# A decoder trunk in one kernel: a depthwise convolution split between TensorE and VectorE, a swish without GpSimd, and modulation work moved to an earlier stage

## The chip, the cores and the metric

The kernel runs on one core of one Trainium2 chip. The metric is the device time of one launch in microseconds (us), here the median of the runs of one kernel. TensorE (PE in the rows, its weight loads PEld) multiplies, VectorE (DVE), ScalarE (ACT) and GpSimd (POOL) do the elementwise work, and SyncE (SP) issues nearly all DMA transfers.

## The reference

The sequence has 256 tokens of 2048 channels. Layer 0 mixes tokens with a state-space mixer (S5), layer 1 with a Conformer convolution; a SwiGLU network of width 5632 follows each. Every sub-layer gets its shift, scale and gate from a projection of one conditioning vector `c` (the modulation).

```python
for i in range(DEPTH):                                   # 2 layers
    mod = c_act @ ada_w[i] + ada_b[i]                    # 2048 x 12288: six vectors of 2048
    h = x * (1.0 + sc_m) + sh_m
    y = s5_mixer(h, ...) if i % 2 == 0 else conv_mixer(h, ...)
    x = layer_norm(ALPHA * x + (1.0 + gt_m) * y, ...)
    h = x * (1.0 + sc_f) + sh_f
    y = swiglu_ffn(h, ffn_w_gu[i], ffn_w_down[i])
    x = layer_norm(ALPHA * x + (1.0 + gt_f) * y, ...)

def conv_mixer(u, w_pw1, w_dw, b_dw, g_norm, b_norm, w_pw2):
    ab = u @ w_pw1
    v = ab[..., :d] * jax.nn.sigmoid(ab[..., d:])
    v = depthwise causal convolution of v, 31 taps per channel, + b_dw
    v = layer_norm(v, g_norm, b_norm)                    # over the channels
    return jax.nn.silu(v) @ w_pw2
```

## The kernel before

**Units.** Every weight matrix goes through the same path (class `Unit`, `gemm`). A unit is 1 MB of weights, 4 blocks of 128 rows by 512 columns, loaded by SyncE into one of four `raw` buffers. ScalarE casts it to `whi` (L830) and VectorE subtracts to get the remainder `wlo` (L831); both have two buffers. TensorE then runs 24 products of 512 columns (L884) or 48 of 256 columns (L888), those with `whi` first and those with `wlo` last. A unit's casts can start when the unit two places earlier has been multiplied.

**Modulation.** `AdaQueue` works through the 2048 x 12288 matrices beside the units: at each unit `ada.rate` is added to a credit, and at 1.0 one step is taken: a load of 1 MB into another `raw` buffer (L684) and a multiply-add of 128 x 2048 on VectorE (L699). `ada.hold` stops it. There are 128 such steps in all.

**The convolution stage** multiplies by `cv_w_pw1` in eight groups of four units; group i gives channel chunks 2i and 2i+1 (128 channels each). Group 0 is done by `entry.panel`, groups 1 to 7 by `gemm`. When a group is ready, `conv_in` writes it zero-padded to `pad`, sends it to a scratch in DRAM (L1542) and reads it back four times shifted (`vs`, L1557); GpSimd makes the tap matrices `lw` (L1547). `conv_out` (L1574) computes a chunk with 32 products of 256 columns; fp32 products have two instructions each in the trace, so 64 rows a chunk. VectorE takes the result from PSUM to `V`, with the bias added and a shift subtracted (L1583). The last group has no time for DRAM: `conv_spread` (L1564) copies and shifts it with TensorE, into PSUM banks that ScalarE (L1566) and VectorE (L1568) empty in turn. Spreads and convolutions share three banks (tag `aux`). What is to run some units later is put into a list (`later.put(n, ...)`, n units ahead).

**Normalisation and swish.** `Stats` sums `V` and its squares (`lnsq`) over the chunks on VectorE (L773, L775), and `finish` sums over the partitions on TensorE (`lnsum`). Then `Feed` runs beside the first product with `cv_w_pw2` (q = 0, four units, L888): for each pair of chunks `swish` normalises on VectorE (L818, L819), takes the sigmoid and the affine on ScalarE (L1611, L945), multiplies on GpSimd (L1613), rounds to the high part on VectorE (L908) and takes the low part on GpSimd (L909). TensorE waits for these parts pair by pair.

The instructions of each engine are put in a fixed order when the program is built, and each engine works through its own in that order.

Of the kernel before, what the change touches and what calls it, by code (L numbers as in the profile page):

```python
# [26 lines left out]
CONV_G = 8  # L27
WIDTH = 31
# [477 lines left out]
def kernel(  # L506
# [231 lines left out]
    class Stats:  # L738
# [22 lines left out]
        def add(self, i, z):  # L761

            sq = self.sp.tile([P, 2, SEQ], F32, tag="lnsq", name="lnsq", bufs=2)
            act = nc.scalar.activation(out=sq, in_=z, func=AF.Square)
# [7 lines left out]
            a, b = self.first if i == 1 else (s[:, 0], s[:, 1])  # L772
            dve = nc.vector.tensor_tensor(out=s[:, 0], in0=a, in1=z, op=ADD)  # L773
            if i < 7:
                nc.vector.tensor_tensor(out=s[:, 1], in0=b, in1=sq, op=ADD)  # L775
            else:
                self.tail = sq
                self.marks = [dve, act]

        def finish(self, fill=None):  # L780
# [4 lines left out]
            sp, s, sq = self.sp, self.s, self.tail  # L785
# [5 lines left out]
            for k in range(2):  # L791
                for q in range(4):
                    t = slice(64 * q, 64 * q + 64)
                    mm = nc.tensor.matmul(b[32 * q:32 * q + 32, 64:P], ones[:, 0:32], sq[:, k, t], start=False, stop=k == 1)
# [567 lines left out]
    const2 = wp = ln_col = wtap = fold32 = row_of = None  # L1362

# [71 lines left out]
    def load_vectors():  # L1435
# [18 lines left out]
        later.put(4, lambda: turn_vectors(ab, ln, rt))  # L1454

# [20 lines left out]
    with mctx:  # L1476
# [39 lines left out]
        ada.rate, ada.behind = 0.71, True  # L1516
# [11 lines left out]
        for p in pad:  # L1528
            nc.vector.memset(p[:, :, :WIDTH - 1], 0.0)
            nc.vector.memset(p[:, :, LP - 1:], 0.0)  # L1530
        dramp = cvctx.enter_context(tc.tile_pool(name="dram", bufs=1, space=bass.MemoryType.DRAM))
        scr = [dramp.tile([P, 2, LP], F32, name=f"scr{i}") for i in range(7)]
        cstats = Stats("cln", sp)
        ada.rate = 0.6

        def conv_in(i, t):
            p = pad[i % 2]
            for k in range(2):
                nc.scalar.copy(out=p[:, k, WIDTH - 1:LP - 1].rearrange("p (c t) -> p t c", t=2), in_=t[:, k].rearrange("p (t c) -> p t c", t=2))
            vs = cp.tile([P, 2, 4, LS], F32, tag="vs", name="vs", bufs=2)  # L1540
            if i < 7:
                later.put(3, lambda: nc.sync.dma_start(scr[i], p))  # L1542
                later.put(4, lambda: conv_copies(scr[i], vs))
            for k in range(2):
                ch = 2 * i + k
# [23 lines left out]

        def conv_out(ch, vs, lw):  # L1570
            acc = aux("conv")[:, :SEQ]
            for g in range(CONV_G):
                for q in range(4):
                    nc.tensor.matmul(  # L1574
                        acc[32 * q:32 * q + 32, :], lw[:, q, g, :], vs[:, q, 4 * g:4 * g + SEQ], start=g == 0, stop=g == CONV_G - 1)
# [9 lines left out]
            if ch % 2 == 1:  # L1585
                cstats.add(ch // 2, V[:, ch - 1:ch + 1])
# [6 lines left out]
        def swish(i, r):  # L1593
            s2 = slice(2 * i, 2 * i + 2)
            if i == 0:
                h = sp.tile([P, 2, SEQ], F32, tag="hf", name="hf", bufs=2)
                for ch in range(2):
# [6 lines left out]
                    nc.gpsimd.tensor_tensor(out=hl[:, ch], in0=h[:, ch], in1=hh[:, ch].bitcast(F32), op=SUB)  # L1604
# [8 lines left out]
            nc.gpsimd.tensor_tensor(out=h, in0=h, in1=V[:, s2], op=MUL)  # L1613
# [64 lines left out]
```

## Time and profile before

| | before |
|---|---|
| median of 3 runs | 2331.22 us (2330.57 to 2331.48) |
| the profiled execution | 2333.25 us, of it a span of 2331.5 us |
| TensorE busy | 2258.8 us, 97% |
| VectorE busy | 1637.7 us, 70% |
| ScalarE, GpSimd busy | 1009.7 us and 234.6 us |
| convolution stage, groups 1 to 7 | about 1215 to 1417 us of the span |
| its last convolutions, sums | about 1417 to 1442 us |
| swish beside the first product with `cv_w_pw2` | about 1447 to 1487 us |
| first feed-forward network | about 420 to 1170 us |

All stretches below are microseconds from the start of the span. A row of the timeline has its start, its time (of a row with a count, from the first start to the last end), the engine, line, operation, what is written and read, and in brackets the idle time just before and what ended it. Instructions on VectorE and ScalarE overlap a little: three equal ones in a row take less than three times one.

### The profile page before, as it was taken

The numbers are of one execution on the slowest core, as the hardware profiler recorded it, in microseconds if no ns is written. First come the engines' busy times: TensorE is split into PE (matmuls) and PEld (weight loads), VectorE is DVE, ScalarE is ACT, GpSimd is POOL, SyncE is SP. The second block draws the span as 40 slices with busy tenths as digits, with TensorE's granted clock in tenths as the row PEclk, the third lists the DMA queues.
The fourth block names the chain that finished last, engine by engine and source line by source line (L and its number), as shares of the span: only waits on it lengthen the run. The fifth ranks groups of instructions, "written<-read, shape, count | busy, mean of one in ns | idle before, by whom it ended". The sixth has DMA issues, their size and how long they took to land.

```text
span 2331.5 us, 34014 instructions
## 1 busy us (share of the span) xinstructions
PE 2258.8 (97%) x13905; PEld 1818.0 (78%) x13905; DVE 1637.7 (70%) x1754; ACT 1009.7 (43%) x1242; POOL 234.6 (10%) x307
## 2 busy tenths in 40 slices
PE   7888999999999999999999998999999999999998
PEld 4545777888888888888887776797888888888888
DVE  8899888877776777777884656788755444455564
ACT  4665334644333333434463322556433433334343
POOL 5662000200000000000030111302000000000000
PEclk8999999999999999999999999999999999999999
DMA  9888898489888888988748886765865555555552
GB/s 334 300 295 294 293 334 293 163 307 320 298 320 295 311 314 305 323 294 304 271 145 243 260 244 213 264 218 182 279 225 181 194 185 193 186 181 190 188 164 90
DMA packets 382307, 582.36 MB, mean 250 GB/s; under 512 B 13603, under 2 KB 279123, under 8 KB 367683
## 3 DMA queue, kind: packets, MB, share of 16 engines
q1 hardware_dynamic: 381718, 579.73, 73.6%
q8 instruction: 109, 1.79, 0.3%
q0 software_dynamic: 192, 0.37, 0.1%
q14 instruction: 48, 0.39, 0.0%
q10 hardware_dynamic: 240, 0.08, 0.0%
HBM read 575.97 MB, written 4.15 MB: 249 GB/s over the span
## 4 chain that ended last, share of the span: by engine, by line
PE 76%; DVE 9%; issue 5%; DMA 4%; ACT 3%; POOL 2%; SPq 1%; DVEq 0%; POOLq 0%; ACTq 0%
PE acc L884 66%; PE acc L888 3%; PE conv L1574 2%; DVE wlo L831 2%; PE turned L900 2%; DMA raw<-in_s_w_glu_dram 1%; DVE pin L462 1%; ACT whi L830 1%; POOL h L982 1%; PE y L499 1%; DVE adaacc L699 1%; DMA raw<-in_cv_w_pw_dram 1%; DMA vs<-scr 1%; DVE x L450 1%; DVE pin L450 1%
## 5 line engine op out<-in xcount | busy, mean ns | idle before, releaser
L831 DVE TENSOR_TENSOR wlo<-raw,whi 128x2048 fp32r<-128x2048 f32 x344 | 797.7, 2319 | 510.1 <-ACT whi L830 510.0
L830 ACT CAST whi<-raw 128x2048 fp32r<-128x2048 f32 x344 | 654.8, 1904 | 806.2 <-PE acc L884 533.4
L884 PE MATMUL acc<-whi,h 128*128 128x512 f32 x3648 | 901.1, 396 | 15.7 <-ACT whi L830 15.3
L884 PEld LDWEIGHTS acc<-whi,h 128*128 128x128 f32 x3648 | 682.5, 189 | 175.9 <-ACT whi L830 20.8
L884 PE MATMUL acc<-wlo,h 128*128 128x512 f32 x1824 | 465.0, 392 | 1.9 <-DVE wlo L831 1.7
L884 PEld LDWEIGHTS acc<-wlo,h 128*128 128x128 f32 x1824 | 342.1, 188 | 79.5 <-DVE wlo L831 4.4
L884 PE MATMUL acc<-whi,f 128*128 128x512 f32 x1248 | 300.5, 391 | 0.0
L699 DVE SCALAR_TENSOR_TENSOR adaacc<-rawa,c_act,adaacc 128x2048 f32<-128x2048 f32 (+1 forms) x135 | 286.8, 2124 | 1.1 <-DMA rawa<-in_ada_w_dram 0.7
L884 PEld LDWEIGHTS acc<-whi,f 128*128 128x128 f32 x1248 | 233.0, 188 | 49.0 <-ACT whi L830 0.8
L884 PE MATMUL acc<-wlo,f 128*128 128x512 f32 x624 | 156.6, 389 | 0.8 <-DVE wlo L831 0.8
L884 PEld LDWEIGHTS acc<-wlo,f 128*128 128x128 f32 x624 | 117.0, 188 | 25.5 <-DVE wlo L831 1.3
L1547 POOL TENSOR_TENSOR lw<-fold,wtap 128x1024 f32<-128x1024 f32 x16 | 33.9, 2122 | 889.7 <-PE acc L888 711.7
L982 POOL TENSOR_TENSOR h<-hf,h 128x512 fp32r<-128x512 f32 x24 | 48.2, 2016 | 333.7 <-ACT h L981 326.5
L1207 ACT ACTIVATE fsg<-acc 128x256 f32<-128x256 f32 x84 | 31.9, 380 | 102.4 <-PE acc L884 102.3
L628 PE MATMUL ada<-raw,c_rep 128*32 128x512 f32 (+1 forms) x576 | 71.5, 593 | 4.0 <-DMA raw<-in_ada_w_dram 3.9
L1153 POOL CAST lnmh<-lno 128x2 fp32r<-128x2 f32 x1 | 0.2, 181 | 713.5 <-DVE lno L66 713.5
L888 PEld LDWEIGHTS acc<-h,whi 128*128 128x128 f32 x512 | 63.4, 194 | 8.0 <-DVE h L1603 2.1
L888 PE MATMUL acc<-h,whi 128*128 128x256 f32 x512 | 66.9, 286 | 2.5 <-DVE h L1603 1.1
L1574 PE MATMUL conv<-vs,lw 128*32 128x256 f32 x1024 | 60.8, 380 | 0.4 <-DMA vs<-scr 0.3
L1574 PEld LDWEIGHTS conv<-vs,lw 128*32 128x32 f32 x1024 | 34.9, 110 | 23.8 <-issue 3.6
L1208 DVE TENSOR_TENSOR fsg<-acc,fsg 128x256 f32<-128x256 f32 x84 | 35.3, 420 | 19.6 <-ACT fsg L1207 19.5
L462 DVE TENSOR_TENSOR_SCAN pin<-rho,pin 128x256 f32<-128x256 f32 x64 | 44.3, 692 | 1.5
(331 smaller groups left out, 1846.0 us busy)
## 6 DMA issues: line engine op xcount, KB each, us to landing
raw<-in_ffn_w_gu_dram SPq DMA_DIRECT2D x352, 512.0 KB, 4.5
rawa<-in_ada_w_dram SPq DMA_DIRECT2D x128, 1024.0 KB, 6.4
raw<-in_ffn_w_down_dram SPq DMA_DIRECT2D x88, 1024.0 KB, 5.1
raw<-in_ada_w_dram SPq DMA_DIRECT2D x64, 1024.0 KB, 8.0
raw<-in_s_w_glu_dram SPq DMA_DIRECT2D x64, 512.0 KB, 6.0
raw<-in_cv_w_pw_dram SPq DMA_DIRECT2D x64, 512.0 KB, 6.7
raw<-in_cv_w_pw_dram SPq DMA_DIRECT2D x16, 1024.0 KB, 5.6
vs<-scr SPq DMA_DIRECT2D x28, 284.0 KB, 7.2
```

Of the source, the lines that this page charges most:

```text
L450: self.end = v.tensor_tensor(out=o, in0=i, in1=bc(t[:, k, a::2], 1, 4), op=MUL)
L462: v.tensor_tensor_scan(out=z, data0=rh[:, a].rearrange("p r h c -> p (r h c)"), data1=z, initial=0.0, op0=MUL, op1=ADD)
L628: nc.tensor.matmul(acc[32 * (k % 4):32 * (k % 4) + 32, :], c_rep[:, kk, :], r[:, k, :], start=kk < 4, stop=kk >= NCH - 4)
L699: nc.vector.scalar_tensor_tensor(out=acc, in0=r[:, i], scalar=c_act[:, kk:kk + 1], in1=acc, op0=MUL, op1=ADD)
L830: m1 = nc.scalar.copy(out=self.hi[:, :kn], in_=r[:, :kn])
L831: m2 = nc.vector.tensor_tensor(out=self.lo[:, :kn], in0=r[:, :kn], in1=self.hi[:, :kn].bitcast(F32), op=SUB)
L884: nc.tensor.matmul(acc[bank].rearrange("p a b -> p (a b)"), x[:, bank * HALF:(bank + 1) * HALF], wt[:, k], start=first, stop=end)
L888: nc.tensor.matmul(acc[bank][:, i], wt[:, k, m * P:(m + 1) * P], x, start=first and i == 0, stop=end and i == 1)
L900: nc.tensor.transpose(b[:, o:o + HALF], u[t][:, c0 + k * P:c0 + (k + 1) * P], ident)
L982: nc.gpsimd.tensor_tensor(out=hl[:, s2], in0=h, in1=hh[:, s2].bitcast(F32), op=SUB)
L1208: nc.vector.tensor_tensor(out=t[:, i], in0=gv[:, 0], in1=t[:, i], op=MUL)
L1574: nc.tensor.matmul(acc[32 * q:32 * q + 32, :], lw[:, q, g, :], vs[:, q, 4 * g:4 * g + SEQ], start=g == 0, stop=g == CONV_G - 1)
```

## The change

Chunks 3, 7, 11 and 13 are convolved wholly on VectorE, one multiply-add of 128 x 256 per tap (`conv_taps`): 31 taps in two alternating sums (`vacc` and the chunk's place in `V`), then one addition and one subtraction of the shift. Of chunk 15, taps 8 to 30 go to VectorE and taps 0 to 7 stay on TensorE (`conv_rest`, 8 products instead of 32). The taps are spread over later units, 4 a unit for chunks 3 and 7, 7 for chunk 11, 9 for chunk 13, and 23 at once for chunk 15. Chunks 3, 7, 11 and 13 need no `lw`, no scratch and no `vs`. Their tap columns are loaded and turned once, far ahead (`tap_columns`). The modulation rate goes from 0.71 to 0.77 in the first feed-forward network and from 0.6 to 0.25 in the convolution stage, with none from group 6 on. The swish loses GpSimd: VectorE multiplies and takes the low part, ScalarE rounds. The last pair of chunks is no longer added to the sums by VectorE; TensorE sums it apart.

```diff
+V_CHUNKS = (3, 7, 11, 13, 15)
+V_FROM = 8
...
             if i < 7:
                 nc.vector.tensor_tensor(out=s[:, 1], in0=b, in1=sq, op=ADD)
             else:
-                self.tail = sq
-                self.marks = [dve, act]
+                self.tail = None, sq
...
+            for o, a in ((0, z), (64, sq)):
+                for k in range(2 if a is not None else 0):
+                    for q in range(4):
+                        t = slice(64 * q, 64 * q + 64)
+                        mm = nc.tensor.matmul(b[32 * q:32 * q + 32, o:o + 64], ones[:, 0:32], a[:, k, t], start=False, stop=o + k == 65)
...
+    def tap_columns():
+
+        for n, chunks_ in enumerate((V_CHUNKS[:4], V_CHUNKS[4:])):
+            r = rows_in("taps", [cv_w_dw[0][:, P * c:P * c + P] for c in chunks_], nc.gpsimd)
+            t = turned_rows(f"taps{n}", r, const2)
+            for i, c in enumerate(chunks_):
+                taps[c] = t[:, WIDTH * i:WIDTH * (i + 1)]
...
-        ada.rate, ada.behind = 0.71, True
+        ada.rate, ada.behind = 0.77, True
...
-        for p in pad:
+        vpad = [cp.tile([P, 1, LP], F32, name=f"vpad{i}") for i in range(2)]
+        for p in pad + vpad:
...
-        cstats = Stats("cln", sp)
-        ada.rate = 0.6
+        cstats = Stats("cln", sp, True)
+        ada.rate = 0.25
...
+                if k == 1 and mine:
+                    later.put(4, lambda v=v, lw=lw: conv_rest(v, lw))
+                else:
+                    later.put((2 if i == 7 else 6) + k, lambda k=k, v=v, lw=lw: conv_out(ch + k, v, lw))
+            if not mine:
+                return
+            acc = cp.tile([P, SEQ], F32, tag="vacc", name="vacc", bufs=2)
+            todo = list(range(V_FROM if i == 7 else 0, WIDTH))
+            n = {5: 7, 6: 9, 7: 23}.get(i, 4)
+            for m in range(0, len(todo), n):
+                later.put(1 + m // n, lambda js=todo[m:m + n]: conv_taps(ch + 1, acc, z[1], js, todo[0], js[-1] == WIDTH - 1))
...
+        def conv_taps(ch, acc, z, js, begin, last):
+
+            w, sums = taps[ch], (acc, V[:, ch])
+            for j in js:
+                a = sums[j % 2]
+                if j == begin:
+                    nc.vector.tensor_scalar(out=a, in0=z[:, j:j + SEQ], scalar1=w[:, j:j + 1], scalar2=cb_col[:, ch:ch + 1], op0=MUL, op1=ADD)
+                elif j == begin + 1:
+                    nc.vector.tensor_scalar(out=a, in0=z[:, j:j + SEQ], scalar1=w[:, j:j + 1], scalar2=None, op0=MUL)
+                else:
+                    nc.vector.scalar_tensor_tensor(out=a, in0=z[:, j:j + SEQ], scalar=w[:, j:j + 1], in1=a, op0=MUL, op1=ADD)
+            if not last:
+                return
+            nc.vector.tensor_tensor(out=acc, in0=acc, in1=V[:, ch], op=ADD)
...
+        def conv_rest(vs, lw):
+
+            acc = aux("conv")[:, :SEQ]
+            conv_groups(acc, vs, lw, V_FROM // 4)
...
         for i in range(8):
+            ada.hold = i > 5
...
-                    nc.gpsimd.tensor_tensor(out=hl[:, ch], in0=h[:, ch], in1=hh[:, ch].bitcast(F32), op=SUB)
+                    nc.vector.tensor_tensor(out=hl[:, ch], in0=h[:, ch], in1=hh[:, ch].bitcast(F32), op=SUB)
...
-            nc.gpsimd.tensor_tensor(out=h, in0=h, in1=V[:, s2], op=MUL)
-            return [m1] + split3(h, hh[:, s2], hl[:, s2])
+            nc.vector.tensor_tensor(out=h, in0=h, in1=V[:, s2], op=MUL)
+            return split(h, hh[:, s2], hl[:, s2])
```

**The end of the convolution on VectorE.** These are VectorE's instructions in their order, from the last gate of group 7 (`sg`) to the sums, in the kernel before; `vs<-spread` empties a spread's bank, `V<-conv` a convolution's.

```order
L1062 TENSOR_TENSOR sg<-acc,sg 128x256 x2
L1568 COPY vs<-spread 128x284 x2
L1583 SCALAR_TENSOR_TENSOR V<-conv,vec,shift 128x128x2
L1568 COPY vs<-spread 128x284 x2
L1583 SCALAR_TENSOR_TENSOR V<-conv,vec,shift 128x128x2
L773 TENSOR_TENSOR cln_s<-cln_s,V 128x512
```

The same place in the changed kernel, where `...` stands for 20 more taps of chunk 15, `vacc` and `V` in turn.

```order
L1060 TENSOR_TENSOR sg<-acc,sg 128x256
L1628 COPY vs<-spread 128x284
L1587 TENSOR_SCALAR vacc<-pad_10111,taps_4091,vec 128x256
L1589 TENSOR_SCALAR V<-pad_10111,taps_4091 128x256
L1591 SCALAR_TENSOR_TENSOR vacc<-pad_10111,taps_4091,vacc 128x256
L1628 COPY vs<-spread 128x284
...
L1646 SCALAR_TENSOR_TENSOR V<-conv,vec,shift 128x128x2
L1594 TENSOR_TENSOR vacc<-vacc,V 128x256
L1628 COPY vs<-spread 128x284
L1596 TENSOR_TENSOR vacc<-vacc,shift 128x256
```

Twenty taps have come between the second bank of the first spread and the result of chunk 14, and the banks of the second spread are emptied only after them.

**The swish on VectorE.** These are VectorE's instructions beside the first product with `cv_w_pw2`, from the first `wlo` of that stretch on, in the kernel before (`V<-V,lnrep` normalises, `h<-hf` rounds).

```order
L831 TENSOR_TENSOR wlo<-raw,whi 128x2048
L818 TENSOR_TENSOR V<-V,lnrep 128x512
L908 CAST h<-hf 128x2x256
L819 TENSOR_TENSOR V<-V,lnrep 128x512
L908 CAST h<-hf 128x2x256
L831 TENSOR_TENSOR wlo<-raw,whi 128x2048
L908 CAST h<-hf 128x2x256 x2
```

And in the changed kernel.

```order
L834 TENSOR_TENSOR wlo<-raw,whi 128x2048
L908 TENSOR_TENSOR h<-hf,h 128x2x256
L822 TENSOR_TENSOR V<-V,lnrep 128x512
L821 TENSOR_TENSOR V<-V,lnrep 128x512
L822 TENSOR_TENSOR V<-V,lnrep 128x512
L1676 TENSOR_TENSOR hf<-hf,V 128x512
L834 TENSOR_TENSOR wlo<-raw,whi 128x2048
L908 TENSOR_TENSOR h<-hf,h 128x2x256
```

Where one rounding stood for each pair, a multiplication and a subtraction stand now, and the last `wlo` of the stretch comes before the last subtraction.

**The loads of the convolution stage.** These are SyncE's transfers in the middle of that stage before: `raw` is a weight load, two to a unit, `rawa` a modulation step, `scr` and `vs` the way through DRAM.

```order
L1557 DMA vs<-scr_10062 32x8x284 x4
L584 DMA raw<-in_cv_w_pw_dram 128x4x256 x2
L684 DMA rawa<-in_ada_w_dram 128x2048
L584 DMA raw<-in_cv_w_pw_dram 128x4x256 x4
L1542 DMA scr_10063<-pad_10051 128x574
L684 DMA rawa<-in_ada_w_dram 128x2048
```

The same place in the changed kernel.

```order
L586 DMA raw<-in_cv_w_pw_dram 128x4x256
L686 DMA rawa<-in_ada_w_dram 128x2048
L586 DMA raw<-in_cv_w_pw_dram 128x4x256 x2
L1556 DMA scr_10127<-pad_10111 128x287
L586 DMA raw<-in_cv_w_pw_dram 128x4x256 x2
L1617 DMA vs<-scr_10127 32x4x284 x4
```

Modulation loads in this stage go from 13 to 2; ten of the others stand in the first feed-forward network now (89 there instead of 79) and one in the second. A group with a chunk on VectorE sends half as much through DRAM.

## Rows read from the trace of the kernel before

**Rows 1.** The page, part 1: busy time, share of the span, instructions

```profile
PE 2258.8 (97%) x13905; PEld 1818.0 (78%) x13905; DVE 1637.7 (70%) x1754; ACT 1009.7 (43%) x1242; POOL 234.6 (10%) x307
```

**Rows 2.** Busy time by stretch: the header names the columns

```profile
core 0: us, PE busy (x) PEld busy (x) DVE busy (x) ACT busy (x) POOL busy (x), PEclk, DMA share, GB/s
520.00:1020.00 500.00, 500.00 (x2258) 407.84 (x2257) 374.04 (x255) 192.77 (x145) 0.00 (x0) 1.00 0.88 310
1215.00:1417.00 202.00, 198.51 (x1526) 150.04 (x1527) 122.44 (x82) 71.92 (x81) 29.06 (x14) 0.99 0.80 243
1240.00:1440.00 200.00, 193.72 (x1747) 142.47 (x1746) 111.81 (x81) 57.58 (x62) 27.40 (x13) 1.00 0.79 236
1447.00:1487.00 40.00, 32.98 (x236) 26.73 (x235) 28.70 (x42) 23.34 (x36) 25.48 (x16) 0.91 0.79 283
```

**Rows 3.** The timeline near the end of the convolution, TensorE

```profile
1385.72 3.93 PE L888 MATMUL acc<-h,whi 128*128 128x256 f32 x32
...
1391.91 7.11 PE L1574 MATMUL conv<-vs,lw 128*32 128x256 f32 x128
...
1418.01 2.12 PE L1564 MATMUL spread<-pad,ident 128*32 128x284 f32 x32 [0.56 <-ACT pad L1539]
...
1440.41 0.95 PE L790 MATMUL lnsum<-cln_s,ones 128*32 128x128 f32 x16 [2.25 <-DVE cln_s L775]
```

**Rows 4.** VectorE in 1240 to 1440 by groups: count, busy us, mean ns, idle before

```profile
L831 DVE TENSOR_TENSOR wlo<-raw,whi 128x2048 fp32r<-128x2048 f32 x22 | 57.4, 2611 | 35.0 <-ACT whi L830 35.0
L699 DVE SCALAR_TENSOR_TENSOR adaacc<-rawa,c_act,adaacc 128x2048 f32<-128x2048 f32 x11 | 27.9, 2534 | 0.0
L1583 DVE SCALAR_TENSOR_TENSOR V<-conv,vec,shift 128x256 f32<-128x256 f32 x14 | 9.7, 690 | 46.8 <-PE conv L1574 46.8
L775 DVE TENSOR_TENSOR cln_s<-cln_s,lnsq 128x512 f32<-128x512 f32 x5 | 3.4, 682 | 0.0
```

**Rows 5.** A group of 1530 to 1565, then the timeline: four such instructions together

```profile
L967 DVE SCALAR_TENSOR_TENSOR raw<-X,f1g,raw 128x256 fp32r<-128x256 f32 x16 | 7.0, 481 | 0.2 <-ACT raw L966 0.2
...
1533.18 1.68 DVE L967 SCALAR_TENSOR_TENSOR raw<-X,f1g,raw 128x256 fp32r<-128x256 f32 x4 [0.20 <-ACT raw L966]
```

**Rows 6.** The timeline: VectorE's remainder beside GpSimd's tap matrix, and one alone

```profile
1399.20 2.00 POOL L1547 TENSOR_TENSOR lw<-fold,wtap 128x1024 f32<-128x1024 f32 x1 [1.49 <-PE conv L1574]
...
1399.62 3.72 DVE L831 TENSOR_TENSOR wlo<-raw,whi 128x2048 fp32r<-128x2048 f32 x1
...
1344.38 2.28 DVE L831 TENSOR_TENSOR wlo<-raw,whi 128x2048 fp32r<-128x2048 f32 x1
```

**Rows 7.** TensorE behind an idle stretch, and without one; the clock by stretch

```profile
1214.99 5.54 PE L884 MATMUL acc<-whi,h 128*128 128x512 f32 x16 [2.60 <-ACT whi L830]
...
1522.94 3.94 PE L884 MATMUL acc<-whi,h 128*128 128x512 f32 x16
...
1215.00:1219.00 4.00, 4.00 (x11) 3.16 (x12) 4.00 (x6) 3.77 (x8) 1.55 (x1) 0.57 0.00 0
```

**Rows 8.** The timeline of the swish: its first, some middle and its last instructions

```profile
1447.52 0.42 DVE L818 TENSOR_TENSOR V<-V,lnrep 128x256 f32<-128x256 f32 x1 [1.93 <-PE lnrep L809]
...
1462.26 1.29 POOL L909 TENSOR_TENSOR h<-hf,h 128x512 fp32r<-128x512 f32 x1 [0.54 <-DVE h L908]
...
1463.52 3.33 POOL L1613 TENSOR_TENSOR hf<-hf,V 128x512 f32<-128x512 f32 x1
...
1478.49 2.28 DVE L831 TENSOR_TENSOR wlo<-raw,whi 128x2048 fp32r<-128x2048 f32 x1
...
1486.21 1.07 PE L888 MATMUL acc<-h,whi 128*128 128x256 f32 x8
```

**Rows 9.** The swish's stretch, 1447 to 1487, by groups, as in rows 4

```profile
L831 DVE TENSOR_TENSOR wlo<-raw,whi 128x2048 fp32r<-128x2048 f32 x4 | 9.9, 2464 | 0.0
L908 DVE CAST h<-hf 128x512 fp32r<-128x512 f32 x7 | 3.0, 428 | 10.6 <-POOL hf L1613 10.6
L1611 ACT ACTIVATE hf<-V,vec 128x256 f32<-128x256 f32 x14 | 7.7, 593 | 7.5 <-POOL h L909 5.3 <-DVE V L819 2.2
```

More of the change, by code (lines that the diff above doesn't have):

```diff
@@ L763, in add @@
             sq = self.sp.tile([P, 2, SEQ], F32, tag="lnsq", name="lnsq", bufs=2)
-            act = nc.scalar.activation(out=sq, in_=z, func=AF.Square)
+            nc.scalar.activation(out=sq, in_=z, func=AF.Square)
             s = self.s
@@ L1362 @@
     const2 = wp = ln_col = wtap = fold32 = row_of = None
+    taps = {}
     def scan(ct, now, y):
@@ L1532 @@
         scr = [dramp.tile([P, 2, LP], F32, name=f"scr{i}") for i in range(7)]
-        cstats = Stats("cln", sp)
-        ada.rate = 0.6
+        cstats = Stats("cln", sp, True)
+        ada.rate = 0.25
+        done = set()
         def conv_in(i, t):
-            p = pad[i % 2]
+            own = i in (1, 3, 5)
+            p, z = pad[i % 2], [pad[i % 2][:, 0], vpad[i // 2 % 2][:, 0] if own else pad[i % 2][:, 1]]
             for k in range(2):
-                nc.scalar.copy(out=p[:, k, WIDTH - 1:LP - 1].rearrange("p (c t) -> p t c", t=2), in_=t[:, k].rearrange("p (t c) -> p t c", t=2))
-            vs = cp.tile([P, 2, 4, LS], F32, tag="vs", name="vs", bufs=2)
+                nc.scalar.copy(out=z[k][:, WIDTH - 1:LP - 1].rearrange("p (c t) -> p t c", t=2), in_=t[:, k].rearrange("p (t c) -> p t c", t=2))
+            ch = 2 * i
+            mine = ch + 1 in V_CHUNKS
+            vs = [cp.tile([P, 4, LS], F32, tag="vs", name="vs", bufs=3) for _ in range(1 if mine and i < 7 else 2)]
             if i < 7:
-                later.put(3, lambda: nc.sync.dma_start(scr[i], p))
+                later.put(3, lambda: nc.sync.dma_start(scr[i][:, :len(vs)], p[:, :len(vs)]))
                 later.put(4, lambda: conv_copies(scr[i], vs))
-            for k in range(2):
-                ch = 2 * i + k
+            for k, v in enumerate(vs):
                 lw = cp.tile([P, 4, CONV_G, 32], F32, tag="lw", name="lw", bufs=3)
@@ new lines, in conv_in @@
+            if i == 7:
+                tail.append(acc)
+        tail = []
+        def conv_taps(ch, acc, z, js, begin, last):
[11 more added lines that the diff above has]
+            nc.vector.tensor_tensor(out=acc, in0=acc, in1=V[:, ch], op=ADD)
+            o, shift = acc.rearrange("p (c t) -> p c t", t=2), cstats.shift.rearrange("p (t c) -> p c t", t=2)
+            nc.vector.tensor_tensor(out=V[:, ch].rearrange("p (t c) -> p c t", t=2) if ch < 15 else o, in0=o, in1=shift, op=SUB)
+            if ch < 15:
+                there(ch)
@@ L1554, in conv_copies, with there @@
+        def conv_rest(vs, lw):
+            acc = aux("conv")[:, :SEQ]
+            conv_groups(acc, vs, lw, V_FROM // 4)
+            o, a, b = V[:, 15].rearrange("p (t c) -> p c t", t=2), *(x.rearrange("p (c t) -> p c t", t=2) for x in (acc, tail[0]))
+            nc.vector.tensor_tensor(out=o, in0=a, in1=b, op=ADD)
+            there(15)
+        def there(ch):
+            done.add(ch)
+            if ch ^ 1 in done:
+                cstats.add(ch // 2, V[:, ch & ~1:(ch | 1) + 1])
         def conv_copies(s, vs):
@@ L1627 @@
         feed = Feed(cstats, swish, fill())
+        ada.hold = False
         ada.finish(1, 2)
```

37 lines of the change are left out of this document (16 added, 21 removed).

## The prediction

> **What bounds the kernel now.** I read the page's busy shares first. TensorE is busy 97% of the span and VectorE 70% [rows 1], so a microsecond of TensorE work that goes to VectorE should come off the time wherever VectorE has room and is not late. That is a question for each stage, so I read the busy times by stretch next [rows 2]. In groups 1 to 7 of the convolution TensorE is busy 198.5 of 202 us and VectorE 122.4. In the first feed-forward network TensorE never stops (500.0 of 500), VectorE is busy 75%, and the transfer engines 0.88. The swish's stretch is different: TensorE 33.0 of 40, and three other engines between 23 and 29. The change thus touches a stage that TensorE bounds and one that a chain of small hand-offs bounds.
>
> **Term 1, three whole chunks off TensorE: -10.7 us.** Two chunks take 7.11 us [rows 3], one 3.55. Chunks 3, 7 and 11 were convolved before the last product of group 7 ended: 3 x 3.55 = 10.7. Chunks 13 and 15 belong to the tail (term 3).
>
> **Term 2, VectorE in the stage: 0, between -3 and +5.** The nearest row to a tap is the multiply-add of L967: same operation, 128 x 256, both tensors in SBUF, a column as the scalar. One takes 0.481 us, but four in a row 1.68 [rows 5], so each starts 0.08 before the last one ends and costs 0.40. The 147 taps (4 x 31 + 23) cost 147 x 0.40 = 59 us. Between 1240 and 1440 VectorE is now busy 111.8 us [rows 2]. Out of it go eleven of thirteen modulation steps, 27.9 us by their group [rows 4], less 3 for the two kept: -25. Out go five evacuations, 5 x 0.69, and the last pair's two sums, 2 x 0.68: -4.8. In come, beside the taps, five additions and five subtractions at no more than 0.6: +5. That makes 87 + 59 = 146 us in some 189, or 77%. The room is there on average. It is not there everywhere: up to 18 taps (7.2 us) stand between two `wlo`, where before a `wlo` waited for ScalarE (35.0 us in all [rows 4]). A unit's buffer is free one unit (5.6 us) before its `whi` products start, and its `wlo` products start 3.8 us later (16 of 24 products); casting and subtracting take 1.9 + 2.2, so VectorE may be 5 us late before TensorE waits. I count small waits, which the eleven loads taken out of this stage pay back: TensorE idles 3.5 us here now [rows 2], the most there is to win, and one late `wlo` in each group would cost about 5.
>
> **Term 3, the tail: 0, between -6.2 and +3.** TensorE's own work falls by one and three quarter chunks, 1.75 x 3.55 = 6.2 us, and this would be the gain if TensorE stayed the last. I think it doesn't. Before, group 7's first product starts at 1385.7 and the sums over partitions at 1440.4 [rows 3], 54.7 us. After, VectorE's list decides. Its `wlo` for the third unit can't end before 5.7 (first unit multiplied [rows 3]) + 1.9 + 2.2 = 9.8 us. Behind it stand, in this order up to chunk 14's evacuation: 54 taps (chunk 13's 31, as 18 + 2 + 5 + 1 + 3 + 2, and chunk 15's 23), 54 x 0.40 = 21.6; two `wlo`, 4.4; two evacuations and two sums, 4 x 0.61 = 2.4; and six short ones (two gates, two copies, an addition, a subtraction) at 0.4, 2.4. The evacuation ends at 9.8 + 30.8 = 40.6. Only then does chunk 14 give its bank to the second spread: TensorE still has half a spread (2.12 / 2 [rows 3]), chunk 12 (3.55), and behind it VectorE an evacuation and three additions at 0.61. That gives 40.6 + 1.1 + 3.6 + 2.4 = 47.7, 7.0 less than before, of which 3.6 is chunk 11, already in term 1. So 3.4 us of the 6.2 would be left. Two things eat it. The tap matrix of chunk 15 falls into this list: beside one a `wlo` took 3.72 us instead of 2.28 [rows 6], +1.4. And TensorE now stands still for 4 us while it waits for the bank. [...] Together 0, with -6.2 (VectorE never last) and +3 (its list 3 us later) as ends.
>
> [...] The row of four says 0.40, and I go by the row.
>
> **Term 4, the swish without GpSimd: -5 us, between -9 and 0.** From the first normalisation at 1447.5 to the end of the product at 1487.3 are 39.8 us [rows 8]. VectorE's roundings waited 10.6 us for GpSimd there, and ScalarE 5.3 [rows 9]; beside a `wlo` a multiplication on GpSimd took 3.33 instead of about 1.3 us [rows 8]. Without GpSimd VectorE has the first pair, 14 instructions of 256 columns at up to 0.34 = 4.8; seven pairs with four instructions of 512 columns at 0.60 = 16.8; and four `wlo` at 2.2 = 8.8: 30.4 us. ScalarE has 23.3 now [rows 2] and seven roundings more at about 0.6: 27.5. Each pair goes VectorE, ScalarE, VectorE, ScalarE, VectorE, and the last one also behind a `whi` and a `wlo`, so the list won't run without gaps. I add 3.4 us of gaps (bounds 0 and 9.4; at 9.4 nothing is won), and TensorE's last eight products, 1.1 [rows 8]: 34.9 us, 5 less.
>
> **Term 5, ten modulation steps more in the first network: +0.5, between 0 and +4.** A step is 1.05 MB. At 310 GB/s and a share of 0.88 [rows 2] the engines would move 352 GB/s when full, so ten steps are 30 us of transfers; 500 us at 0.88 leave 60 free, and the network has 750. VectorE gets 10 x 2.3 = 23 us, of which a quarter of 750 is free. Both lie beside TensorE; if half the steps delayed a `whi` by 1 us past its slack, it would be 4.
>
> **Term 6, small work: +1.0.** TensorE sums the last pair by 16 more rows like those of `lnsum` (under 0.95 for 16 wider ones [rows 3]); turning the tap columns, and four fills on VectorE, have no row of their own and are shorter than that. Nothing waits for the tap loads: three units of products stand between the buffer's release and their use.
>
> Sum: -10.7 + 0 + 0 - 5 + 0.5 + 1.0 = -14.2. The profiled execution took 2333.25 us, so 2319.05; it lies 2.0 above the median of the runs, so the median after comes to 2317.0 us.
>
> **The rivals.** The likeliest case holds the time between 2312 and 2322; I give it 0.55.
>
> (a) VectorE keeps up in the tail and TensorE's 6.2 us come off whole, and the stage's 3 us of waits go too: 2317 - 9.2 = 2308. For it: the idle time before evacuations, 46.8 us [rows 4]. Against it: the list above, 40.6 us long. 0.13.
>
> (b) The swish gains nothing, because two engines now carry what three did, and the feed-forward network pays its 4: 2317 + 5 + 3.5 = 2325.5; with one of the two, 2321 to 2322 and just above. 0.17.
>
> (c) Bursts of taps make TensorE wait in most groups and the tail loses its 3: the gain shrinks to within 0.2%, about 2330. 0.08.
>
> (d) VectorE becomes the bound of the whole stage, and the kernel is slower. The price decides it: VectorE has 87 us of other work there, so 147 taps fill the 189 us at 0.69 each, and at 0.77 the stage is as long as before. If a tap had to wait until the one before it was done and written, at 0.48 + 0.40 = 0.88, the stage would need 87 + 129 = 216 instead of 200: +16 - 5 + 0.5 + 1.0 = +12.5, or 2343.7. Against it: the four of rows 5, which do overlap. For it: a `wlo` held for 1.4 us by a tap matrix [rows 6]; nine tap matrices remain in the stage, and 9 x 1.4 = 13 us would raise a tap to only 0.49. 0.07. [...]
>
> **How the numbers follow.** A difference of 0.2%, 4.7 us, is about what a measurement of this kernel can tell from none, so faster means below 2326.6: the likeliest case, (a) and (b), 0.85. Same is (c), 0.08; slower is (d), 0.07. The range from 2308 to 2326 leaves out half of (a)'s lower side, (c) and (d).
>
> **What would show it.** A tap that follows a tap costs 0.40, and VectorE is busy 77% in the stage. The last product of group 7 ends about 11 us earlier. In the tail TensorE waits 4 us, with chunk 14's evacuation on VectorE as what ended the wait, at a lowered clock behind it; if that wait is missing, term 3 is wrong by up to 6. In the swish the stretch from the first normalisation to the product's end is 35 us long. Between 520 and 1020 TensorE still shows 100%. The prediction fails if a tap costs above 0.5, or if the `wlo` behind the bursts hold TensorE by more than 1 us a group.

## The result, and the profile after

The changed kernel takes 2334.35 us (median of 20 runs) against 2330.47 us before, a ratio of 1.0016 (95% interval 1.0009 to 1.0022). I had forecast 2317.0 us, faster, in a range from 2308 to 2326. The profiled execution after took 2331.15 us, with a span of 2329.0. One of the 20 runs, 5663.39 us, counts in the median and not in the ratio. The two profiled executions lie the other way round (2331.15 after, 2333.25 before), so stage times read from them, here and below, can be off by about three us in all.

The first line of the page, beside [rows 1]:

```profile
PE 2261.3 (97%) x13619; PEld 1804.6 (77%) x13619; DVE 1694.1 (73%) x1921; ACT 1014.2 (44%) x1249; POOL 204.0 (9%) x292
```

TensorE has 286 recorded instructions fewer and is not a microsecond less busy. So work did leave TensorE, and something took the time back. The busy times by stretch, of three stretches of [rows 2] (the swish's stretch begins 8 us earlier now), have the columns that their header names:

```profile
core 0: us, PE busy (x) PEld busy (x) DVE busy (x) ACT busy (x) POOL busy (x), PEclk, DMA share, GB/s
520.00:1020.00 500.00, 499.81 (x2224) 400.74 (x2223) 381.84 (x257) 188.74 (x142) 0.00 (x0) 1.00 0.91 320
1240.00:1440.00 200.00, 191.31 (x1553) 140.88 (x1552) 153.98 (x241) 59.64 (x66) 19.48 (x9) 0.97 0.62 179
1439.00:1479.00 40.00, 34.24 (x252) 28.01 (x251) 36.06 (x54) 28.85 (x44) 0.00 (x0) 0.96 0.88 316
```

In the first network TensorE is as full as before, yet it passes 2224 products in 500 us where it passed 2258 at the same clock, 1.00. VectorE is busy 77% of 1240 to 1440, as forecast. To find where time goes, I compared the starts of the sums over partitions (`lnsum`), one set at the end of each stage, in the two traces. The one ahead of the first network comes 3.2 us earlier after the change (419.3 against 422.5), the one behind it 7.3 later (1187.6 against 1180.3), the one behind the convolution 7.5 earlier (1432.9 against 1440.4), the next 11.6 earlier (1552.2 against 1563.8), the last two 3.1 and 2.1 earlier. So the convolution gained 14.8 us (10.7 forecast) and the swish's stage 4.1 (5 forecast), while the first network lost 10.5 and the second, in which only one modulation step is new, lost 8.5.

In the first network the loss has hardly a wait in it: TensorE waits 0.2 us in all between 470 and 1180. These are two units of the group of products ahead of the convolution, before (first) and after, from the timeline of TensorE: start, length of the row, products.

```profile
1227.69 3.83 PE L884 MATMUL acc<-whi,h 128*128 128x512 f32 x16
1231.35 1.99 PE L884 MATMUL acc<-wlo,h 128*128 128x512 f32 x8
1233.18 3.83 PE L884 MATMUL acc<-whi,h 128*128 128x512 f32 x16
```

```profile
1240.06 3.90 PE L887 MATMUL acc<-whi,h 128*128 128x512 f32 x16
1243.79 2.03 PE L887 MATMUL acc<-wlo,h 128*128 128x512 f32 x8
1245.66 3.90 PE L887 MATMUL acc<-whi,h 128*128 128x512 f32 x16
```

24 products took 5.49 us (0.2288 each) and take 5.60 (0.2333). Over all products of `h` the starts are mostly about 0.2290 apart before and 0.2333 after. A second kind of product did not change at all, those whose loaded operand is the gated product `f`. Two rows of them, before (first) and after:

```profile
715.68 1.98 PE L884 MATMUL acc<-wlo,f 128*128 128x512 f32 x8
717.49 3.79 PE L884 MATMUL acc<-whi,f 128*128 128x512 f32 x16
```

```profile
718.95 1.98 PE L887 MATMUL acc<-wlo,f 128*128 128x512 f32 x8
726.67 1.98 PE L887 MATMUL acc<-whi,f 128*128 128x512 f32 x8
```

Eight of them go by in 1.81 us, 0.226 each (717.49 - 715.68), and rows of eight are 1.98 long after as before. It is the same instruction on the same weights' tiles at the same clock (1.00 in 520 to 1020, both); only the loaded operand is another.

One thing that differs is where the operands lie. The built program has `h` at byte 38272 of each partition in both kernels. The tiles `whi` lie at 113344 and 121536 before, and 640 bytes higher after, because the two tap-column tiles (496 and 124 bytes, 512 and 128 with padding) stand in the pool ahead of them. `f` lies behind the weights and moved with them. **Theory A:** the spacing depends on the distance between streamed weights and loaded chunks; there are 5472 such products (3648 + 1824 in the page's groups), and 5472 x 0.0043 = 24 us. **Rival B:** the change's work (more transfers in the network, VectorE's bursts) slows TensorE.

### The profile page after: what moved, and what is told of

Read it like the earlier page. It is cut to its first block, busy times and chain, and to the rows that moved or that the text cites. A ratio compares the mean times of both kernels' runs of the same rounds, so it can differ in the third digit from the quotient of the medians.

```text
span 2329.0 us, 33641 instructions
## 1 busy us (share of the span) xinstructions
PE 2261.3 (97%) x13619; PEld 1804.6 (77%) x13619; DVE 1694.1 (73%) x1921; ACT 1014.2 (44%) x1249; POOL 204.0 (9%) x292
## 4 chain that ended last, share of the span: by engine, by line
PE 80%; DVE 9%; ACT 4%; issue 3%; DMA 2%; POOL 1%; SPq 0%; DVEq 0%; ACTq 0%; POOLq 0%
PE acc L887 68%; PE acc L891 4%; PE turned L903 2%; ACT whi L833 1%; PE conv L1633 1%; DVE wlo L834 1%; DVE pin L464 1%; DMA raw<-in_s_w_glu_dram 1%; PE y L501 1%; POOL h L980 1%; PE acc L997 1%; DVE x L452 1%; DMA raw<-in_ada_w_dram 1%; DVE pin L452 1%; DVE V L1591 0%
## 5 line engine op out<-in xcount | busy, mean ns | idle before, releaser
L834 DVE TENSOR_TENSOR wlo<-raw,whi 128x2048 fp32r<-128x2048 f32 x344 | 789.6, 2296 | 476.3 <-ACT whi L833 470.2
L887 PE MATMUL acc<-whi,h 128*128 128x512 f32 x3648 | 915.8, 399 | 12.5 <-ACT whi L833 12.4
L887 PE MATMUL acc<-wlo,h 128*128 128x512 f32 x1824 | 472.5, 395 | 0.5 <-DVE wlo L834 0.5
L1560 POOL TENSOR_TENSOR lw<-fold,wtap 128x1024 f32<-128x1024 f32 x12 | 26.0, 2171 | 882.2 <-PE acc L891 722.2
L1633 PE MATMUL conv<-vs,lw 128*32 128x256 f32 x720 | 45.0, 400 | 2.5 <-DVE V L1646 2.0
L1633 PEld LDWEIGHTS conv<-vs,lw 128*32 128x32 f32 x720 | 23.4, 115 | 22.6 <-issue 6.5
```

The source lines that it names most:

```text
L834: m2 = nc.vector.tensor_tensor(out=self.lo[:, :kn], in0=r[:, :kn], in1=self.hi[:, :kn].bitcast(F32), op=SUB)
L887: nc.tensor.matmul(acc[bank].rearrange("p a b -> p (a b)"), x[:, bank * HALF:(bank + 1) * HALF], wt[:, k], start=first, stop=end)
L1633: nc.tensor.matmul(acc[32 * q:32 * q + 32, :], lw[:, q, g, :], vs[:, q, 4 * g:4 * g + SEQ], start=g == 0, stop=g == n - 1)
```

## The experiments

Each kernel's ratio is to the kernel before, timed beside it on the same chip (2329.3 us for experiments 1, 2 and 7, 2329.85 for 4, for the old rates in 5 and for the pieces in 8, 2329.44 for the rest).

**1. The kernel before, 640 bytes moved.**

```diff
         later.put(4, lambda: turn_vectors(ab, ln, rt))
+        gap = const2.tile([P, 160], F32, name="gap")
+        nc.gpsimd.memset(gap[:, 0:1], 0.0)
```

> The kernel before with one unused tile of 640 bytes a partition in the pool ahead of the weight buffers, as much room as the tap columns take in the changed kernel; nothing else is edited. The weights' rounded and remainder tiles, and all that lies behind them, move 640 bytes up; the input chunks of the products don't. Theory A (the changed kernel lost its gain because its 512-column products of the input chunks are started every 0.2333 us instead of every 0.2290, and this comes from where the weights lie in SBUF against the chunks): every such product takes 0.2333 here too; there are 5472 of them, 5472 x 0.0043 = 24 us, so about 2354 against 2330.5. Rival B (the spacing comes from the change's work: loads moved ahead, VectorE's bursts, the order of the queues): 0.2290 and 2330.5, no change.

Measured: 2348.28 us, ratio 1.0084 (1.0071 to 1.0098), 19 us slower by one unused tile. Three rows of its timeline, TensorE:

```profile
1232.06 3.90 PE L884 MATMUL acc<-whi,h 128*128 128x512 f32 x16
1235.79 2.03 PE L884 MATMUL acc<-wlo,h 128*128 128x512 f32 x8
1237.66 3.90 PE L884 MATMUL acc<-whi,h 128*128 128x512 f32 x16
```

5.60 us for 24: the changed kernel's spacing, with none of its work. So the displacement is enough to make it, and Rival B is not needed. 19 of the 24 us show; where the other 5 went was not followed up.

**2. The changed kernel with the tap columns in the convolution's pool,** so that the weights lie where they lay.

```diff
-        later.put(5, tap_columns)
...
-            t = turned_rows(f"taps{n}", r, const2)
+            t = turned_rows(f"taps{n}", r, cp)
...
         done = set()
+        later.put(1, lambda: tap_columns(cp))
```

> The changed kernel, but the two tiles of tap columns are loaded and turned at the start of the convolution and live in that stage's own pool, so that the weights' tiles lie where they lay before the change. Theory A: the spacing is 0.2290 again, and the time falls by 24 us to about 2310 against 2334.35 of the changed kernel. Rival B: 0.2333 and about 2334. Rival C (the spacing costs nothing because other waits take its place): spacing 0.2290 but above 2325.

Measured: 2318.13 us, ratio 0.9951 (0.9938 to 0.9963), spacing 0.2290. With all of the change's work in place the spacing is that of before, so Rival B falls. Theory A holds again, but 8 us short of what it expected. Against the changed kernel that is 16 us less by the medians and 15 by the ratios. By the starts of the sums its convolution takes 17.4 us less than before, the swish's stage 5.2 less and the second network nothing, but the first network still 7.5 more. That is another loss, followed up in 5 and 6.

**3. The distance by itself.** This program only multiplies constant tiles, with no transfer and no other engine at work meanwhile:

> No part of the reference is computed; the output is zeros. 84 units of 24 products of 512 columns, in the order of a unit of the kernel, on constant tiles, with no transfer and no other engine at work. The first 4 units warm up. In the next 32 the streamed weights' start moves up by 64 bytes from unit to unit, in the next 32 the start of the loaded (stationary) chunks, and in the last 16 both move by 128 bytes together. Theory A, in the form that the two addresses collide: the time of a unit changes with either offset, between about 5.44 us (0.2267 a product) and 5.60 (0.2333) or more, with a period, and stays level in the last 16. A', only one address matters: level in one of the two groups of 32 and moving in the last 16. Rival B: 5.4 us everywhere.

Rows of its timeline: streamed weights moved by 0, 64, 128, 192 and 256 bytes (first five), loaded chunks by 0, 64, 128, 192 and 256 (next five), both together (last three). At 0 they lie 10240 bytes apart, a multiple of 256. A unit lasts from one row's start to the start of the next unit.

```profile
33.82 3.79 PE L38 MATMUL even<-hi,st 128*128 128x512 f32 x16
...
39.26 3.84 PE L38 MATMUL odd<-hi,st 128*128 128x512 f32 x16
...
44.77 3.89 PE L38 MATMUL even<-hi,st 128*128 128x512 f32 x16
...
50.35 3.90 PE L38 MATMUL odd<-hi,st 128*128 128x512 f32 x16
...
55.96 3.81 PE L38 MATMUL even<-hi,st 128*128 128x512 f32 x16
...
211.08 3.81 PE L38 MATMUL even<-hi,st 128*128 128x512 f32 x16
...
216.54 3.90 PE L38 MATMUL odd<-hi,st 128*128 128x512 f32 x16
...
222.13 3.88 PE L38 MATMUL even<-hi,st 128*128 128x512 f32 x16
...
227.71 3.84 PE L38 MATMUL odd<-hi,st 128*128 128x512 f32 x16
...
233.22 3.80 PE L38 MATMUL even<-hi,st 128*128 128x512 f32 x16
...
404.51 3.79 PE L38 MATMUL odd<-hi,st 128*128 128x512 f32 x16
...
409.96 3.79 PE L38 MATMUL even<-hi,st 128*128 128x512 f32 x16
...
415.41 3.79 PE L38 MATMUL odd<-hi,st 128*128 128x512 f32 x16
```

The streamed operand moved up costs 5.44, 5.51, 5.58, 5.61, and 5.46 again at 256; all 32 steps repeat this. The loaded one moved up costs nearly the same in the opposite order, 5.46, 5.59, 5.58, 5.51. Moved together, in steps of 128 bytes, 5.45 throughout. So, in the steps tried, it is the distance, streamed less loaded, modulo 256 bytes: on average 0 gives 0.2272 us a product, 64 gives 0.2296, 128 gives 0.2327, 192 gives 0.2335. The kernel before has 113344 - 38272 = 75072 bytes, 64 past a multiple of 256; the changed one 75712, 192 past; `f` is a multiple of 256 away in both (177088 - 113344 = 63744 = 249 x 256). All three agree with their spacings (0.2290, 0.2333, 0.226) to about 0.001.

**4. The distance made a multiple of 256,** in the changed kernel by 64 bytes (called kernel 4 from here on; the diff) and in the kernel before by 192 (48 columns in place of 16):

```diff
+        gap = const2.tile([P, 16], F32, name="gap")
+        nc.gpsimd.memset(gap[:, 0:1], 0.0)
         later.put(4, lambda: turn_vectors(ab, ln, rt))
```

> The changed kernel with one unused tile of 64 bytes a partition more in the pool ahead of the weight buffers; nothing else is edited. The distance from the input chunks to the weights' tiles becomes 75776 bytes, a multiple of 256 (75712 before this edit, 75072 in the kernel before the change). By the sweep a 512-column product takes 0.2272 us at such a distance, 0.2296 at 64 bytes past one (the kernel before) and 0.2335 at 192 past one (the changed kernel). Theory A: the spacing falls to 0.2270 to 0.2275; 5472 products x 0.006 = 33 us of TensorE time, of which, as in the kernel with the unused 640 bytes (19 us of 24), some four fifths come off the time: about 2308 against 2334. Rival: the kernel's transfers and other engines blur the rule that the sweep showed on an idle core, and the time stays near 2318, that of the kernel with the tap columns in the convolution's pool.

> The kernel before the change with an unused tile of 192 bytes a partition ahead of the weight buffers, so that their distance from the input chunks is a multiple of 256 here too. Theory A: 0.2290 becomes 0.2272; 5472 x 0.0018 = 10 us, four fifths of it 8: about 2321 against 2329.3. Rival: within 2 us of 2329.3.

Measured: 2310.83 us, ratio 0.9927 (0.9913 to 0.9941), and 2321.75, ratio 0.9968 (0.9958 to 0.9978). The spacing falls to 0.227 in both; three rows of the changed kernel with 64 bytes:

```profile
572.40 3.79 PE L887 MATMUL acc<-whi,h 128*128 128x512 f32 x16
576.03 1.98 PE L887 MATMUL acc<-wlo,h 128*128 128x512 f32 x8
577.84 1.98 PE L887 MATMUL acc<-whi,h 128*128 128x512 f32 x8
```

5.44 us for 24. An unused 64 bytes are worth 23.5 us here by the medians and 21 by the ratios, and at equal distance the change is worth 2321.75 - 2310.83 = 10.9 us, near what it gains at the old distance (2329.3 - 2318.1 = 11.2).

Not every product gains. In those of 256 columns `h` is streamed and the weights are loaded. Sixteen of them, with the distance 192 past a multiple of 256 (the kernel of experiment 2, first) and 0 past (kernel 4):

```profile
1446.47 1.98 PE L891 MATMUL acc<-h,wlo 128*128 128x256 f32 x16
```

```profile
1442.40 2.08 PE L891 MATMUL acc<-h,wlo 128*128 128x256 f32 x16
```

Over each trace their starts are mostly 0.113 to 0.119 us apart in the kernels with 64 or 192 past, and 0.119 to 0.121 in the kernels with 0. Those that stream `f`, at a multiple of 256 in every kernel, take 0.120 throughout. For this shape the multiple of 256 is the slowest of the three.

**5. The modulation steps.** The same kernel with the old rates, and the kernel before with the new ones alone:

```diff
-        ada.rate, ada.behind = 0.77, True
+        ada.rate, ada.behind = 0.71, True
...
-        ada.rate = 0.25
+        ada.rate = 0.6
...
-            ada.hold = i > 5
```

> The kernel with the unused 64 bytes, and the modulation steps where they were before the change (rates 0.71 in the first network and 0.6 in the convolution, not held there); the taps and the swish stay changed. Theory: in the kernel with the tap columns in the convolution's pool the first network took 7.5 us longer than before, 1.4 of it a vector's sums moved there and 5.7 the transposes waiting for VectorE; this goes, and the convolution gets 25 us of VectorE work back, on an engine that is busy 77% there. If VectorE has the room: 4 to 6 us faster than the kernel with the unused 64 bytes. Rival (the move is needed): the convolution loses more than that, and the time is the same or up to 15 us longer.

> The kernel before with only the modulation steps moved (rates 0.77 and 0.25, held in groups 6 and 7); all taps stay on TensorE, the swish is the old one, no tile moves. From the traces so far: the first network pays 5 to 8 us (1.4 us of a vector's sums and the transposes' waits for VectorE), the convolution gives back the 1.2 us of sums and at most the 3.5 us that TensorE idles there, since VectorE was busy only 56% there. Theory (the move buys room for the taps and nothing by itself): 2 to 6 us slower than before, 2332 to 2336. Rival (the steps hold up the convolution even without taps): 2 to 5 us faster.

Measured: 2334.32 us, ratio 1.0019 (1.0006 to 1.0032), 23.5 slower than with the steps moved; and 2330.97, ratio 1.0011 (1.0002 to 1.0019), 1.5 to 2.6 slower than before. The rival holds in the first, by more than the 15 us it allowed, and the theory in the second, at or just under its lower end. The move gains nothing by itself, and the taps lose without it. By itself it moves time between stages: the sums start at 421.4, 1187.3 and 1440.0, so the first network takes 8.1 us more than before and the convolution 7.4 less, with every tap still on TensorE. Why the convolution gains more than the 1.2 + 3.5 us expected was not followed up. With the old rates the first network takes 9.6 us less than in kernel 4 and the convolution 35 more. The waits of TensorE there (for whom, us in all, times, longest):

```profile
PE acc L887 <- DVE wlo L834: 15.3, 3, 9.2
PE conv L1635 <- DVE V L1648: 5.2, 1, 5.2
```

VectorE is only 81% busy from 1240 to 1440, and 80% in kernel 4, so its share is not the difference. At the longest wait it is the order: the first of a chunk's taps, the remainder (`wlo`) behind them, and TensorE's products with it.

```profile
1362.04 0.42 DVE L1589 TENSOR_SCALAR vacc<-vpad,taps,vec 128x256 f32<-128x256 f32 x1 [2.23 <-ACT vpad L1553]
...
1379.06 2.27 DVE L834 TENSOR_TENSOR wlo<-raw,whi 128x2048 fp32r<-128x2048 f32 x1
...
1381.38 3.78 PE L887 MATMUL acc<-wlo,h 128*128 128x512 f32 x8 [9.20 <-DVE wlo L834]
```

All 31 taps of chunk 11 stand between the two, and the modulation step only behind the remainder (1381.24). Kernel 4 has the same taps as 14, 7 and 10 with a remainder after each run. So the step rates changed the order in which the built program puts taps and remainders; why, was not followed up.

What the first network pays shows in the kernel of experiment 2. TensorE's waits from 470 to 1180, then VectorE at one of them:

```profile
PE turned L903 <- DVE fsg L1207: 4.3, 6, 1.5
```

```profile
587.06 0.42 DVE L1206 TENSOR_TENSOR fsg<-acc,fsg 128x256 f32<-128x256 f32 x1
587.39 2.34 DVE L701 SCALAR_TENSOR_TENSOR adaacc<-rawa,c_act,adaacc 128x2048 f32<-128x2048 f32 x1
589.65 0.42 DVE L1207 TENSOR_TENSOR fsg<-acc,fsg 128x256 f32<-128x256 f32 x1
```

A modulation step stands between the gate's two multiplications, and the transposes (`turned`) wait for the second, with TensorE's products queued behind them. In kernel 4 it is 6.2 us in seven waits, and with the move alone 4.4 in five. In the changed kernel itself it is 0.2; that its slower products hid it is likely, and not shown.

**6. Half of the move,** on the kernel with 64 bytes and the tail of experiment 8: rates 0.74 and 0.4.

> The kernel with the unused 64 bytes and chunk 15's taps in pieces of 8, with half of the move: rate 0.74 in the first network and 0.4 in the convolution. Theory: the transposes' waits in the first network, 5.9 us in that kernel, fall by about half, and the convolution with some four steps more stays bounded by TensorE (VectorE 77% plus 4 x 2.3 of 200 us = 82%): 0 to 4 us faster than that kernel, 2306 to 2310. Rival: single steps land ahead of a remainder in the stage and cost more than they free: up to 8 us slower.

Measured: 2315.41 us, ratio 0.9937 (0.9924 to 0.9951), 5 slower than the kernel with pieces of experiment 8, as the rival said, but for another reason: the run did not halve the move. The order of the built program shows that steps move by whole vectors: 79 in the first network as before the change, 5 in the convolution, and the seven more that the last projection needs are forced ahead of it. The network's loss is gone (752.7 us, against 753.1 in the kernel before at the same distance and 762.5 with pieces), but one wait stands in the projection:

```profile
PE adar L709 <- DVE adaacc L701: 12.8, 1, 12.8
```

**7. The swish alone,** on the kernel before:

```diff
-            nc.gpsimd.tensor_tensor(out=h, in0=h, in1=V[:, s2], op=MUL)
-            return [m1] + split3(h, hh[:, s2], hl[:, s2])
+            nc.vector.tensor_tensor(out=h, in0=h, in1=V[:, s2], op=MUL)
+            return split(h, hh[:, s2], hl[:, s2])
```

> The kernel before with only the swish's change: the multiplication on VectorE, the rounding on ScalarE, the remainder on VectorE, nothing on GpSimd. No tile moves. The prediction's term 4: 5 us less, 2325.5 against 2330.5, with the stretch from the first normalisation to the product's end 35 us instead of 39.8. Rival: two engines carry what three did, and the stretch stays within 1 us of 39.8: 2330.

Measured: 2325.89 us, ratio 0.9985 (0.9976 to 0.9994), 3.5 us less. First normalisation, VectorE's last subtraction and TensorE's last products:

```profile
1444.42 0.42 DVE L818 TENSOR_TENSOR V<-V,lnrep 128x256 f32<-128x256 f32 x1 [2.28 <-PE lnrep L809]
```

```profile
1477.57 0.68 DVE L905 TENSOR_TENSOR h<-hf,h 128x512 fp32r<-128x512 f32 x1
...
1479.94 1.11 PE L888 MATMUL acc<-h,whi 128*128 128x256 f32 x8
```

That is 36.6 us, 3.2 less than in [rows 8].

**8. The tail.** Chunk 15's taps in pieces of 8, which puts chunk 14's evacuation ahead of ten of them; and chunk 15 whole on TensorE, its tap columns still loaded so that nothing moves (both with the 64 bytes, whose lines are left out here):

```diff
-            n = {5: 7, 6: 9, 7: 23}.get(i, 4)
+            n = {5: 7, 6: 9, 7: 8}.get(i, 4)
```

```diff
-V_CHUNKS = (3, 7, 11, 13, 15)
+V_CHUNKS = (3, 7, 11, 13)
```

> The kernel with the unused 64 bytes, and chunk 15's 23 taps put off in pieces of 8, 8 and 7 in place of one of 23; the scheduler then puts chunk 14's evacuation ahead of nine of these taps. The prediction's term 3 (in the tail TensorE waits for a bank that chunk 14's evacuation frees behind a list of taps, and then runs at a lowered clock): the wait for it, 2.0 us in the changed kernel, and the low clock behind it go, and the time falls by 3 to 5 us below that of the kernel with the unused 64 bytes. Rival: another wait takes their place in the tail (the copies on VectorE, the taps themselves, now late for the last addition), and the two are within 2 us.

> The kernel with the unused 64 bytes, with chunk 15 convolved whole on TensorE and four whole chunks left to VectorE. TensorE gets 48 products of 32 rows back, 48 x 0.056 = 2.7 us, VectorE loses 23 taps, 9.1 us, in the tail, and the wait for chunk 14's bank (2.0 us) goes with them. Theory (in the tail VectorE's list decides, so the taps of chunk 15 buy little): within 2 us of that kernel. Rival (TensorE decides even there): 2.7 us slower or more.

Measured: 2310.3 us, ratio 0.9917 (0.9904 to 0.9930), and 2306.8, ratio 0.9906 (0.9892 to 0.9920), against 0.9927 (0.9913 to 0.9941) of kernel 4. The intervals overlap: the pieces bring 0.5 us by the medians and 2 by the ratios, no clear gain, and not the 3 to 5 expected. TensorE in the tail of the changed kernel (first), of kernel 4 and with pieces:

```profile
1420.89 0.69 PE L1624 MATMUL spread<-pad,ident 128*32 128x284 f32 x8 [0.52 <-ACT vs L1626]
1423.58 7.47 PE L1633 MATMUL conv<-vs,lw 128*32 128x256 f32 x80 [2.01 <-DVE V L1646]
1432.87 0.65 PE L792 MATMUL lnsum<-cln_s,ones 128*32 128x128 f32 x16 [1.81 <-DVE cln_s L778]
```

```profile
1419.56 4.52 PE L1635 MATMUL conv<-vs,lw 128*32 128x256 f32 x80 [2.00 <-DVE V L1648]
```

```profile
1417.70 4.50 PE L1635 MATMUL conv<-vs,lw 128*32 128x256 f32 x80
1424.96 0.64 PE L792 MATMUL lnsum<-cln_s,ones 128*32 128x128 f32 x16 [2.77 <-DVE cln_s L778]
```

With pieces the wait for the bank goes (2.00 us in kernel 4), and a wait for VectorE's last sum grows in its place (1.80 to 2.77). Kernel 4 has the wait and no slow products behind it: 80 in 4.52 us, near the pace of [rows 3] (128 in 7.11), against 7.47 in the changed kernel, where the granted clock was 0.50 from 1424 to 1429. Giving chunk 15 back to TensorE costs nothing, which fits a tail in which VectorE's list decides. That kernel, 2306.8 us, has the lowest median of all, though its interval overlaps those of kernel 4 and of the pieces; against the kernel before at a multiple of 256 (2321.75) it is 14 to 15 us less.

## Why the prediction was wrong, point by point

**The step that failed is term 6.** I costed the tap columns by turning and loading them, "+1.0", and never asked where they would lie. No rival held it either: (c) named about 2330, but for bursts of taps, and in the changed kernel TensorE waits for no remainder from 1240 to 1440. The displacement costs 19 us by experiment 1, and 15 to 16 in the changed kernel by experiment 2; with the distance of before restored, the changed kernel measures 2318.1 us where I had forecast 2317.0. That agreement is luck in part: there the convolution gained 6.7 us more than forecast (17.4 for 10.7) and the first network lost 7.0 more (7.5 for 0.5). Both misses look like the moved steps, which by themselves do 7.4 and 8.1 (experiment 5).

**Terms 1 and 3, the convolution: near in sum.** The 304 products taken off were 16.9 us of TensorE time; I counted 10.7 and gave the tail nothing. The stage gained 14.8 us as changed and 17.4 with the distance restored (the 576 products of `h` in it cost 2.5). But 7.4 of the 17.4 come with the moved steps alone, where term 2 saw 3.5 as the most there was to win. If the two add up, which no run shows apart, taps and tail brought 10.0, near the 10.7.

TensorE's wait for chunk 14's evacuation is there, 2.0 us where I said 4. VectorE's evacuation ended 39.9 us after group 7's first product (1423.5 - 1383.6; forecast 40.6). The lowered clock came behind it too, 0.54 in 1425 to 1430, and the 80 products there took 7.47 us. It does not follow from that wait alone: kernel 4 has the same wait, 2.00 us, and 4.52 us for the 80. What decides was not found. Term 3 holds 1.6 us for this place, the 5.54 less 3.94 of 16 products of 512 columns in [rows 7]; no run shows that term in the tail, where the 80 products of the changed kernel took 2.95 us more than those of kernel 4. The stretch up to the sums shrank from 54.7 to 49.2 us where I had 51.1, so the tail gave 1.9, and 2.8 at the old distance, instead of 0.

**Term 2, the taps: right in price.** Taps follow each other every 0.396 us (0.40 forecast, from [rows 5]). One tap beside GpSimd's tap matrix took 1.68:

```profile
1405.07 2.85 POOL L1560 TENSOR_TENSOR lw<-fold,wtap 128x1024 f32<-128x1024 f32 x1 [19.21 <-PE conv L1633]
...
1405.60 0.48 DVE L1591 SCALAR_TENSOR_TENSOR vacc<-pad,taps,vacc 128x256 f32<-128x256 f32 x1
1406.00 0.69 DVE L1646 SCALAR_TENSOR_TENSOR V<-conv,vec,shift 128x256 f32<-128x256 f32 x1
1406.52 1.68 DVE L1591 SCALAR_TENSOR_TENSOR V<-pad,taps,V 128x256 f32<-128x256 f32 x1
```

Rival (d), VectorE as the bound of the stage, did not come. Experiment 5 shows another way to lose time to VectorE there, nearer to rival (c): single remainders that come late behind taps while it is 81% busy.

**Term 4, the swish: -5 forecast, -3.5 measured**, inside its bounds. VectorE's list was right: its last subtraction ended 33.8 us after the first normalisation (1478.25 - 1444.42), and 30.4 + 3.4 is 33.8. Behind it TensorE still had 2.8 us of products, where I counted the last eight, 1.1.

**Term 5, the network: +0.5 forecast with 4 as the worst; wrong.** The move alone puts 8.1 us on it. It is 7.5 in experiment 2, and 9.6 in kernel 4 against the kernel before at the same distance (762.7 and 753.1). I looked only at the remainders' slack and at averages. A 2.34 us step in front of the second gate multiplication holds up the transposes, and with them TensorE: 4.4 of the 8.1 us are such waits. 1.4 us are a vector's sums moved there, which the convolution gives back. About 2 us stay open.

## What to carry to other kernels

A new tile is also a displacement: before summing what a change does to the engines, list which operands' addresses it moves, and compare the spacing of equal instructions on differently placed operands. Here the trace of before already had the two spacings, 0.226 for `f` and 0.2290 for `h`, and I read over it. Try such a placement on each shape of product, since what is best for one can be worst for another: the multiple of 256 gave 0.2272 us with 512 columns, the least of the four distances, and 0.120 with 256, the most of three. And an engine's average share says little about bursts: at 80% busy VectorE hardly held a remainder back in the convolution, at 81% in another order that stage took 35 us more. A total that comes out right can hide two misses that cancel, so check a forecast stage by stage.

## What the hardware showed that I had not expected

In a run with a mean granted clock of 0.994 a 128x512 product on TensorE starts every 0.2272, 0.2296, 0.2327 or 0.2335 us as the distance from loaded to streamed operand is 0, 64, 128 or 192 bytes past a multiple of 256; moving both together by 128 bytes changes nothing (experiment 3). 2.8% of the spacing is thus a matter of padding. The 128x256 products of `h` go the other way, 0.120 us at 0 and 0.113 to 0.119 at 64 or 192 (experiment 4); they spread within one distance, so more than the distance is at work, and no sweep was made of them. Distances between multiples of 64, and other shapes, were not tried. Why the distance matters is not shown.
